# Re-ordering the first stage of a hybrid attention block: who sums the adaLN columns, who scales x, and where the gate's sums stand

## The chip, the cores and the metric

The kernel runs on one core of one Trainium2 chip. A core has a matrix engine (TensorE, PE in the profile), three engines for elementwise work (VectorE or DVE, ScalarE or ACT, GpSimd or POOL), and SyncE (SP), whose queue issues every DMA of this kernel. The engines run beside each other and are ordered by semaphores; each engine takes its own instructions strictly in the order in which the program wrote them. The metric is device time in microseconds. The kernel before takes 991.84 us, the median of 3 runs (989.53 to 992.6).

## The reference

One layer on x (1024 tokens by 1024 channels, float32), with a condition vector c of 1024 numbers:

```
ada = c @ w_ada + b_ada;  shift, scale, gate = split(ada, 3)
h = rms_norm(x, norm_w) * (1 + scale) + shift
cq, ckv, k_rope, gate_a, q_b, k_b, v_b, f_b, gate_b, mg_a, mg_b = split(h @ w_in)
branch A: latent attention from rms_norm(cq) @ w_uq and rms_norm(ckv) @ w_ukv, rotary part, chunk mask
branch B: forgetting attention from q_b, k_b, v_b, f_b, causal
merged = sigmoid(mg_a) * (y_a @ w_branch_a) + sigmoid(mg_b) * (y_b @ w_branch_b)
out = x + gate * (merged @ w_out)
```

What the change touches is the first two lines (shift and scale, the normalised and modulated h) and the third part of ada, the gate, which is needed only at the very end.

## The kernel before

Every float32 product is made of three products of a float32r high part and a low part (`hi*hi`, `hi*lo`, `lo*hi`), so each operand is split: ScalarE rounds to the high part, and the low part is a subtraction. h is held transposed, as 8 blocks of 128 channels by 1024 tokens (`hT_hi`, `hT_lo`, index `kt`).

The first stage (`phase0`) loads x in 8 tiles of 128 tokens, squares them with a sum per token, takes a reciprocal square root on VectorE for two tiles at a time (`rsqrt`: 11 small instructions, each needing the one before), and scales the tiles with it (`scale`). Seven of the eight tiles are scaled by GpSimd (L281), one by VectorE (L284). TensorE transposes each scaled tile (`turn`), and ScalarE copies the banks into `xT` (`evac`, L309).

For each channel block the shift and the scale are sums of 1024 products of c with a column of `w_ada`. With the weight's columns on the partitions, such a sum is one 128x1024 multiplication with c, laid along the free dimension of every partition (`cb`), and a sum along it (`ada_cols`). On VectorE it is one instruction (L339). On GpSimd it is the multiplication alone (L342), and ScalarE sums the product later (L344). Before the change the scale's sum of each block is VectorE's and the shift's sums of blocks 2 to 7 are GpSimd's and ScalarE's. The shift of blocks 0 and 1 is a matrix product of TensorE with rows on the partitions (`ada_rows`). `cb` is made by TensorE from a diagonal (`broadcast_c`) and copied by VectorE (L404). `gain` (L348, L349) turns the sums into the block's two per-channel factors `gs`. With them ScalarE writes the high part of h (`high`, L355), VectorE modulates `xT` in place (`modulate`, L359) and subtracts (`low`, L365). Then TensorE does 24 products of 128x424 for the block (`products`, 8 token tiles by 3 parts, into the banks cq_s, cq_o, cq_f, cq_t).

The order of work is written out by hand. In the loop over blocks, iteration `kt` does for block `kt + 1` the sums, the gain and the high part, and for block `kt` modulate, low and the products. The weights of the loads come from a pool of equal pieces of on-chip memory (`Slots`): a load waits, on SP's queue, until the last reader of the piece that it reuses is done.

The gate's 8 sums (`gate_sum`, 128 columns each) use the same form. Before the change they stand at the end of `phase0` and in `latents`: four multiplied by GpSimd (L932) and summed by ScalarE (L936), four by VectorE (L939). `gate_row` transposes the 8 columns to a row and stores it, during `g2q`, the queries of branch A.

After `phase0` come `latents` (the second latent's products, ckv, and their norms), `krope`, `g2q`, then `g2k` (keys and values of branch A, four pairs of token tiles `sp`), the attention of 16 heads, and `output`. From `latents` on, TensorE's time is filled by a planner: `fill_to(t)` puts in products of GEMMs that only have to be done in time (among them branch B's, bank `b`) until the estimated time t.

Of the kernel before, what the change touches and what calls it, by code (L numbers as in the profile page):

```python
# [19 lines left out]
P = 128  # L20
# [21 lines left out]
class Slots:  # L42
    """Equal pieces of SBUF, taken and given back by hand; the one given back longest ago goes first."""
# [31 lines left out]
class Net:  # L75
# [162 lines left out]
    # ------------------------------------------------------------ phase 0  # L238
    def phase0(self):
# [27 lines left out]
        def square(st, engine="a"):  # L267
            junk, a = Hs.get([P, 512], F32, f"junk{st}"), ssq[:, st:st + 1]
            if engine == "a":
                nc.scalar.activation(junk.bitcast(BF16), xs[st], AF.Square, accum_out=a)  # L270
            else:
                nc.vector.scalar_tensor_tensor(out=junk.bitcast(BF16), in0=xs[st], scalar=1.0, in1=xs[st], op0=ALU.mult,
                                               op1=ALU.mult, accum_out=a)
            Hs.put(junk)

        def scale(pair, between=iter(()), engines="pd"):
            a, b = pair
            r = self.rsqrt(ssq[:, a:b + 1], 2, D, f"x{a}", between)
            for i, (st, e) in enumerate(zip(pair, engines)):
                if e == "p":  # L280
                    nc.gpsimd.tensor_scalar(out=xs[st], in0=xs[st], scalar1=r[:, i:i + 1], scalar2=0.0, op0=ALU.mult,  # L281
                                            op1=ALU.add)
                else:
                    nc.vector.tensor_scalar(out=xs[st], in0=xs[st], scalar1=r[:, i:i + 1], scalar2=None, op0=ALU.mult)  # L284
# [20 lines left out]
        def evac(st, engines):  # L305
# [5 lines left out]
        def broadcast_c():  # L311
            """c along the free dimension of every partition, through a diagonal and a product with ones."""
            ones = Hs.get([P, P], F32, "ones")
            nc.gpsimd.memset(ones, 1.0)
            pc = self.bank("s", "cb")
            for g in range(2):
                diag = Hs.get([P, 4, P], F32, f"diag{g}")
                for i in range(4):
                    rc = 4 * g + i
                    nc.vector.tensor_scalar(out=diag[:, i], in0=self.ident, scalar1=col(rc), scalar2=None, op0=ALU.mult)  # L320
                for i in range(4):
                    rc = 4 * g + i
                    self.mm(pc[:, rc * P:(rc + 1) * P], ones, diag[:, i], True, True)
                Hs.put(diag)
            Hs.put(ones)
            return pc

        def ada_rows(kt, bank):
            """The shift of a block whose rows lie on the partitions."""
# [6 lines left out]
        def ada_cols(kt, e, engine="d"):  # L336
            w, a = wada[kt][e], acc[:, kt, e:e + 1]
            if engine == "d":
                nc.vector.scalar_tensor_tensor(out=w, in0=w, scalar=1.0, in1=self.cb, op0=ALU.mult, op1=ALU.mult,  # L339
                                               accum_out=a)  # L340
            elif engine == "p":
                nc.gpsimd.tensor_tensor(out=w, in0=w, in1=self.cb, op=ALU.mult)  # L342
            else:
                nc.scalar.activation(w, w, AF.Copy, accum_out=a)  # L344
# [12 lines left out]
        def modulate(kt, sts=range(ST), engine="d"):  # L357
            c = slice(sts[0] * P, (sts[-1] + 1) * P)
            (nc.vector if engine == "d" else nc.gpsimd).tensor_scalar(  # L359
                out=xT[:, kt, c], in0=xT[:, kt, c], scalar1=gs[:, kt, 1:2], scalar2=gs[:, kt, 0:1],  # L360
                op0=ALU.mult, op1=ALU.add)
# [16 lines left out]
        def modulated(kt, sts):  # L378
            high(kt, sts)
            modulate(kt, sts)  # L380
            low(kt, sts)

# [3 lines left out]
        load(0)  # L386
        load_cq(0, 0)
# [5 lines left out]
        pc = broadcast_c()  # L393
# [18 lines left out]
        wh, wl = U.get([P, 2, 424], F32R, "hi_cq0"), U.get([P, 2, 424], F32R, "lo_cq0")
        nc.scalar.copy(wh[:, 0], cqw[0][:, 0])
        ada_cols(0, 1)
        gain(0, a0)
        high(0, range(4))
        square(6, "d")
        square(7, "d")
        nc.gpsimd.tensor_tensor(out=wl[:, 0], in0=cqw[0][:, 0], in1=wh[:, 0].bitcast(F32), op=ALU.subtract)
        modulate(0, range(4))  # L420
        low(0, range(4))
        self.cqw.append((wh, wl))
        turn(4, "tt")
        evac(4, "aa")
        turn(5, "of")
        evac(5, "aa")
        high(0, (4, 5))
        accs = [self.bank("s", f"cq_s{i}") for i in range(2)]
# [3 lines left out]
        load(2)  # L432
        load_cq(1)
        load(3)
        nc.sync.dma_start(self.misc_raw[:, 0:t["misc"].shape[1]], t["misc"])
        nc.sync.dma_start(self.pos, t["pos"])
        a0 = ada_rows(1, "t")
        products(0, range(4), (2, 1))

        def between():  # L440
            yield
            modulate(0, (4, 5))
            low(0, (4, 5))
            yield

        nc.scalar.copy(wh[:, 1], cqw[0][:, 1])
        nc.gpsimd.tensor_tensor(out=wl[:, 1], in0=cqw[0][:, 1], in1=wh[:, 1].bitcast(F32), op=ALU.subtract)
        U.put(cqw[0])
        ada_cols(2, 0, "p")
        ada_cols(1, 1)  # L450
        gain(1, a0)
        scale((6, 7), between(), "pd")
        high(1, most)
        banks[4], banks[5] = self.bank("o", "cq_o"), self.bank("f", "cq_f")
        products(0, (4, 5), (0, 1))
        modulate(1, most)
        low(1, most)
        products(1, most, (0, ))
        products(0, (4, 5), (2, ))
        products(1, most, (1, ))  # L460
        turn(7, "tt")
        turn(6, "tt")
        products(1, most, (2, ))
        ada_cols(2, 0, "a")
        wh, wl = U.get([P, 2, 424], F32R, "hi_cq1"), U.get([P, 2, 424], F32R, "lo_cq1")
        nc.scalar.copy(wh, cqw[1])
        evac(7, "aa")
        load(4)
        load_cq(2)
        ada_cols(2, 1)  # L470
        gain(2)
        evac(6, "aa")
# [3 lines left out]
        banks[6], banks[7] = self.bank("t", "cq_t0"), self.bank("t", "cq_t1")  # L476
        ada_cols(3, 0, "p")
        load(5)
        for kt in range(2):
            high(kt, last)  # L480
        high(2)
        for kt in range(2):
            modulate(kt, last)
            low(kt, last)
        for kt in range(2):
            products(kt, last)
        ada_cols(4, 0, "p")
        load_cq(3)
        load(6)
        for kt in range(2, KT):  # L490
# [9 lines left out]
            if kt in (3, 5):  # L500
                self.cqw.append(self.split(cqw[(kt + 1) // 2], f"cq{(kt + 1) // 2}"))
            if kt == 3:
                load(7)
            if kt == 4:
                self.kvw = [self.load_w(t["w_ckv"][:, 4 * i:4 * i + 4], [P, 4, 256], f"ckv{i}") for i in range(2)]
            if kt == 5:
                self.gate_load((0, 1))
                self.gate_sum((0, 1), "p")
            if kt == 6:
                self.gate_load((2, 3))  # L510
                self.gate_sum((0, 1), "a")
                self.gate_sum((2, 3), "p")
            if kt == 7:
                self.gate_load((4, 5))
# [1019 lines left out]
```

## Time and profile before

| | |
|---|---|
| median of the runs | 991.84 us (989.53 to 992.6) |
| the profiled execution, span from the first to the last instruction | 989.3 us |
| PE busy | 954.5 us (96%) |
| VectorE busy | 659.8 us (67%) |
| ScalarE busy | 475.7 us (48%) |
| GpSimd busy | 250.8 us (25%) |
| DMA | 123.95 MB, mean 125 GB/s |

The profile gives the profiled execution's span and no separate device time for it; the span is 0.2 us below the fastest run. Busy shares are averages over stages with different limits, so the first stage has to be read by itself: a table of stretches of time, then each engine's instructions in order of time with the idle time before each and what ended it.

### The profile page before, as it was taken

How to read it: one execution, taken by the hardware profiler on the slowest of the kernel's cores; microseconds unless marked ns; L12 is line 12 of the kernel's file. 1: busy time of each engine (PE TensorE's matmuls, PEld its weight loads, DVE VectorE, ACT ScalarE, POOL GpSimd, SP SyncE). 2: the span in 40 equal slices, each digit the busy share in tenths (PEclk: the TensorE clock that was granted, in tenths of full speed). 3: DMA queues.
4: the chain of work that ended last, by engine and by line, in shares of the span. 5: the costliest groups of instructions: out<-in, count | busy, mean ns of one | idle time of the engine just before them, and what ended most of it. 6: DMA issues, size and time to landing. Idle time of an engine off the chain costs nothing.

```text
span 989.3 us, 15335 instructions
## 1 busy us (share of the span) xinstructions
PE 954.5 (96%) x5550; PEld 833.1 (84%) x5550; DVE 659.8 (67%) x1399; ACT 475.7 (48%) x962; POOL 250.8 (25%) x279
## 2 busy tenths in 40 slices
PE   6479999999999999999999999999999999999998
PEld 6379999999998888888888888888888888887887
DVE  6997787676734766757667667677676767495222
ACT  6347653344334655655646566566565644143000
POOL 4843222220001222221223233333332220045000
PEclk9889999999999999999999999999999999999999
DMA  9733113346485223424224232231321554643321
GB/s 345 285 128 131 52 55 107 124 150 221 155 251 149 67 95 84 139 66 109 84 65 119 77 108 66 86 109 65 118 87 45 181 181 148 228 148 126 100 92 64
DMA packets 80700, 123.95 MB, mean 125 GB/s; under 512 B 5896, under 2 KB 47504, under 8 KB 80624
## 3 DMA queue, kind: packets, MB, share of 16 engines
q1 hardware_dynamic: 80624, 122.96, 38.1%
q8 instruction: 44, 0.72, 0.3%
q14 instruction: 32, 0.26, 0.1%
HBM read 87.29 MB, written 35.66 MB: 124 GB/s over the span
## 4 chain that ended last, share of the span: by engine, by line
PE 85%; DVE 8%; DMA 4%; issue 1%; ACT 1%; SPq 0%; POOL 0%; ACTq 0%; DVEq 0%; POOLq 0%
PE f L127 31%; PE b L127 12%; PE out L127 9%; PE s L127 8%; PE o L127 7%; PE pt L136 6%; PE q L127 3%; PE ckv L127 2%; PE kv L127 2%; DVE hT_lo L1046 1%; DVE hT_lo L365 1%; DMA ks_u<-ka_d 1%; DVE wada_u L339 1%; PE cq_s L127 1%; DVE xT L359 1%
## 5 line engine op out<-in xcount | busy, mean ns | idle before, releaser
L1240 ACT CAST pp_u<-pt 128x512 fp32r<-128x512 f32 x192 | 92.1, 480 | 181.6 <-PE pt L136 167.8
L1241 DVE TENSOR_TENSOR pp_u<-pt,pp_u 128x512 fp32r<-128x512 f32 x192 | 106.6, 556 | 79.2 <-ACT pp_u L1240 77.1
L127 PE MATMUL f<-hT_hi,hi_f_u 128*128 128x512 f32 x384 | 153.6, 400 | 0.0
L127 PE MATMUL f<-hT_hi,lo_f_u 128*128 128x512 f32 x384 | 153.4, 400 | 0.0
L127 PE MATMUL f<-hT_lo,hi_f_u 128*128 128x512 f32 x384 | 153.2, 399 | 0.0
L127 PE MATMUL s<-k_u,q_u 96*128 96x512 f32 (+6 forms) x480 | 116.4, 361 | 0.7 <-ACT p_h L1220 0.7
L127 PE MATMUL b<-hi_b_u,hT_hi 128*128 128x256 f32 x384 | 109.6, 285 | 0.0
L127 PE MATMUL b<-hi_b_u,hT_lo 128*128 128x256 f32 x384 | 108.6, 283 | 0.0
L127 PE MATMUL b<-lo_b_u,hT_hi 128*128 128x256 f32 x384 | 108.6, 283 | 0.0
L1224 POOL TENSOR_SCALAR p_u<-p_u,rs 128x640 f32<-128x640 f32 (+1 forms) x64 | 65.2, 1018 | 164.4 <-DVE rs L1223 95.9
L1224 POOL TENSOR_SCALAR p_h<-p_h,rs 128x128 f32<-128x128 f32 (+1 forms) x64 | 38.6, 603 | 245.5 <-DVE rs L1223 205.7
L1214 DVE TENSOR_REDUCE nm<-s 128x1 f32<-128x128 f32 (+7 forms) x128 | 97.0, 758 | 4.4
L127 PE MATMUL o<-pp_u,v_u 128*128 128x512 f32 (+7 forms) x384 | 94.2, 340 | 0.0
L127 PEld LDWEIGHTS f<-hT_hi,lo_f_u 128*128 128x128 f32 x384 | 72.4, 189 | 11.9
L127 PEld LDWEIGHTS f<-hT_lo,hi_f_u 128*128 128x128 f32 x384 | 72.5, 189 | 11.2
L127 PEld LDWEIGHTS f<-hT_hi,hi_f_u 128*128 128x128 f32 x384 | 72.5, 189 | 11.1
L127 PEld LDWEIGHTS s<-k_u,q_u 96*128 96x128 f32 (+2 forms) x480 | 76.7, 190 | 6.1 <-ACT p_h L1220 1.2
L127 PEld LDWEIGHTS o<-pp_u,v_u 128*128 128x128 f32 (+1 forms) x384 | 61.8, 161 | 19.6
L127 PEld LDWEIGHTS b<-lo_b_u,hT_hi 128*128 128x128 f32 x384 | 73.6, 192 | 0.3
L127 PEld LDWEIGHTS b<-hi_b_u,hT_hi 128*128 128x128 f32 x384 | 73.6, 192 | 0.3
L127 PEld LDWEIGHTS b<-hi_b_u,hT_lo 128*128 128x128 f32 x384 | 73.6, 192 | 0.0
L136 PEld LDWEIGHTS pt<-ident,p_u 128*128 128x128 f32 x416 | 52.7, 140 | 16.6
(319 smaller groups left out, 2072.0 us busy)
## 6 DMA issues: line engine op xcount, KB each, us to landing
raw_f_u<-in_w_t SPq DMA_DIRECT2D x24, 512.0 KB
wada_u<-in_w_ada SPq DMA_DIRECT2D x16, 512.0 KB
mg_d<-th_h SPq DMA_DIRECT2D x32, 256.0 KB
mg_h<-mg_d SPq DMA_DIRECT2D x32, 256.0 KB
raw_b_u<-in_w_b SPq DMA_DIRECT2D x12, 512.0 KB
x_u<-in_x SPq DMA_DIRECT2D x8, 512.0 KB
raw_wg_u<-in_w_gate SPq DMA_DIRECT2D x8, 512.0 KB
va_d<-vhl_u SPq DMA_DIRECT2D x8, 512.0 KB
```

The costliest lines, as they stand in the source:

```text
L127: self.nc.tensor.matmul(out, lhsT=l, rhs=r, start=start, stop=stop)
L136: self.nc.tensor.transpose(out=out, in_=in_, identity=self.ident)
L339: nc.vector.scalar_tensor_tensor(out=w, in0=w, scalar=1.0, in1=self.cb, op0=ALU.mult, op1=ALU.mult, accum_out=a)
L359: (nc.vector if engine == "d" else nc.gpsimd).tensor_scalar(out=xT[:, kt, c], in0=xT[:, kt, c], scalar1=gs[:, kt, 1:2], scalar2=gs[:, kt, ...
L365: nc.vector.tensor_tensor(out=lo[:, kt, c], in0=xT[:, kt, c], in1=hi[:, kt, c].bitcast(F32), op=ALU.subtract)
L1046: nc.vector.tensor_tensor(out=self.hT_lo[x], in0=mA[c1][:, x[2]], in1=self.hT_hi[x].bitcast(F32), op=ALU.subtract)
L1214: nc.vector.tensor_reduce(out=nm, in_=sv, axis=AX.X, op=ALU.max, negate=True)
L1224: nc.gpsimd.tensor_scalar(out=p[:, 0:w], in0=p[:, 0:w], scalar1=rs, scalar2=0.0, op0=ALU.mult, op1=ALU.add)
L1240: nc.scalar.copy(ph[:, c0:], pt[:, c0:])
L1241: nc.vector.tensor_tensor(out=pl[:, c0:], in0=pt[:, c0:], in1=ph[:, c0:].bitcast(F32), op=ALU.subtract)
```

## The change

- c's row is laid into `cb` by a DMA with a repeated source row (new input `c_row`); `broadcast_c` and its copy go.
- All shift and scale sums are VectorE's, except block 0's shift (`ada_rows` on TensorE). They are written two blocks ahead of the block's products.
- VectorE scales all 8 tiles of x; all 8 squares are ScalarE's. The low parts of the first weights are VectorE's too, so no GpSimd instruction is left in `phase0` but a memset.
- ScalarE modulates `xT` (Identity with scale and bias, as for the high part) everywhere but for block 0's first six tiles.
- Tiles 6 and 7 of x are scaled, transposed and copied earlier, before block 1's sums.
- The transposes that only keep TensorE's clock up go from 16 to 32.
- The 8 gate sums leave `phase0` and `latents`. They are VectorE's, two behind each pair of `g2k`, with c's row loaded a second time (`cb2`) and the weights loaded one pair ahead. `gate_row` and the bias move into the attention, at head 2, step 0.

```diff
-        def scale(pair, between=iter(()), engines="pd"):
+        def scale(pair):
...
+                nc.vector.tensor_scalar(out=xs[st], in0=xs[st], scalar1=r[:, i:i + 1], scalar2=None, op0=ALU.mult)
...
+            if engine == "a":
+                nc.scalar.activation(xT[:, kt, c], xT[:, kt, c], AF.Identity, scale=gs[:, kt, 1:2], bias=gs[:, kt, 0:1])
+                return
...
+        self.cb = U.get([P, D], F32, "cb")
+        nc.sync.dma_start(self.cb, t["c_row"].broadcast_to([P, D]))
...
-        warm(16, self.ident)
-        scale((0, 1), engines="pp")
+        warm(32, self.ident)
+        scale((0, 1))
         turn(0, "s")
         turn(1, "tt")
...
         a0 = ada_rows(0, "o")
+        evac(2)
+        square(6)
+        ada_cols(0, 1)
+        gain(0, a0)
+        load(2)
+        evac(3)
...
+        high(0, range(4))
+        scale((4, 5))
+        modulate(0, range(4), "d")
         low(0, range(4))
...
+        scale((6, 7))
...
         products(0, range(4), (2, 1))
+        turn(6, "tt")
+        evac(6)
+        turn(7, "tt")
+        modulate(0, (4, 5), "d")
+        low(0, (4, 5))
+        products(0, (4, 5))
+        ada_cols(1, 0)
+        ada_cols(1, 1)
+        gain(1)
+        high(1, most)
+        modulate(1, most, "a")
         nc.scalar.copy(wh[:, 1], cqw[0][:, 1])
+        evac(7)
...
         for kt in range(2, KT):
-            if 2 < kt < KT - 2:
-                ada_cols(kt + 2, 0, "p")
+            if kt + 2 < KT:
+                ada_cols(kt + 2, 0)
+                ada_cols(kt + 2, 1)
+                gain(kt + 2)
             if kt + 1 < KT:
-                ada_cols(kt + 1, 0, "a")
-                ada_cols(kt + 1, 1)
-                gain(kt + 1)
-                high(kt + 1)
-            modulate(kt)
-            low(kt)
+                low(kt + 1)
+            if kt in (2, 4):
+                self.cqw.append(self.split(cqw[kt // 2 + 1], f"cq{kt // 2 + 1}"))
+            if kt + 2 < KT:
+                high(kt + 2)
+                modulate(kt + 2, engine="a")
...
+                self.cb = self.U.get([P, D], F32, "cb2")
+                nc.sync.dma_start(self.cb, t["c_row"].broadcast_to([P, D]))
+                self.gate_load((0, 1))
                 for sp in range(4):
                     self.g2k(sp)
+                    self.gate_sum((2 * sp, 2 * sp + 1))
+                    if sp < 3:
+                        self.gate_load((2 * sp + 2, 2 * sp + 3))
                     self.fill_to(self.pe_time + 6500)
```

## Rows read from the trace of the kernel before

**Rows 1.** Stretches: start:end, length, busy us by engine, PE clock, DMA share, GB/s

```profile
10.50:22.00 11.50, 8.88 (x62) 7.99 (x61) 8.76 (x28) 7.35 (x15) 7.42 (x6) 0.85 1.02 384
22.00:50.00 28.00, 13.50 (x83) 11.85 (x81) 27.44 (x35) 11.95 (x20) 23.12 (x10) 0.89 0.79 292
50.00:58.20 8.20, 8.09 (x32) 7.73 (x33) 8.10 (x17) 4.76 (x7) 0.00 (x0) 0.74 0.31 104
58.20:70.40 12.20, 7.90 (x42) 7.42 (x40) 12.17 (x8) 2.98 (x5) 11.06 (x4) 1.00 0.55 189
87.50:206.00 118.50, 118.39 (x990) 117.84 (x989) 93.36 (x279) 63.59 (x126) 34.56 (x52) 1.00 0.30 98
206.00:272.00 66.00, 66.00 (x466) 62.02 (x466) 46.35 (x118) 27.47 (x49) 4.39 (x5) 1.00 0.48 173
272.00:885.00 613.00, 610.67 (x3331) 514.31 (x3330) 407.97 (x826) 329.46 (x694) 149.92 (x179) 1.00 0.37 114
```

**Rows 2.** TensorE in order of time: start, us, instructions [idle before, releaser]

```profile
18.91 2.51 PE L127 MATMUL pada<-vec,wada_u 128*128 128x64 f32 x16
50.11 1.08 PE L127 MATMUL cq_t<-hi_cq_u,hT_lo 128*128 128x424 f32 x2 [9.14 <-DVE hT_lo L365]
53.10 1.48 PE L127 MATMUL cq_s<-hi_cq_u,hT_hi 128*128 128x424 f32 x4
70.46 1.04 PE L127 MATMUL cq_s<-hi_cq_u,hT_lo 128*128 128x424 f32 x4 [4.36 <-DVE hT_lo L365]
78.27 0.93 PE L127 MATMUL cq_s<-hi_cq_u,hT_hi 128*128 128x424 f32 x4
82.91 0.35 PE L127 MATMUL cq_s<-hi_cq_u,hT_hi 128*128 128x424 f32 x1
87.47 0.28 PE L127 MATMUL ckv<-hi_ckv_u,hT_hi 128*128 128x256 f32 x1
```

**Rows 3.** VectorE in order of time, not held by GpSimd

```profile
33.55 0.75 DVE L284 TENSOR_SCALAR x_u<-x_u,y_x 128x1024 f32<-128x1024 f32 x1
50.76 1.22 DVE L339 SCALAR_TENSOR_TENSOR wada_u<-wada_u,cb_u 128x1024 f32<-128x1024 f32 x1
52.16 0.81 DVE L359 TENSOR_SCALAR xT<-xT,gs 128x1024 f32<-128x1024 f32 x1
53.00 1.23 DVE L365 TENSOR_TENSOR hT_lo<-xT,hT_hi 128x1024 fp32r<-128x1024 f32 x1
54.14 1.22 DVE L339 SCALAR_TENSOR_TENSOR wada_u<-wada_u,cb_u 128x1024 f32<-128x1024 f32 x1
57.53 1.10 DVE L116 TENSOR_TENSOR lo_cq_u<-raw_cq_u,hi_cq_u 128x424 fp32r<-128x424 f32 x2
```

**Rows 4.** VectorE in order of time, the same shapes and one column, while GpSimd works

```profile
38.66 3.40 DVE L339 SCALAR_TENSOR_TENSOR wada_u<-wada_u,cb_u 128x1024 f32<-128x1024 f32 x1
42.12 2.15 DVE L349 SCALAR_TENSOR_TENSOR gs<-ada,b,vec 128x1 f32<-128x1 f32 x1
64.16 2.97 DVE L359 TENSOR_SCALAR xT<-xT,gs 128x1024 f32<-128x1024 f32 x1
67.17 3.24 DVE L365 TENSOR_TENSOR hT_lo<-xT,hT_hi 128x1024 fp32r<-128x1024 f32 x1
```

**Rows 5.** GpSimd in order of time

```profile
14.87 2.22 POOL L281 TENSOR_SCALAR x_u<-x_u,y_x 128x1024 f32<-128x1024 f32 x2 [1.94 <-ACT xT L309]
58.27 11.06 POOL L932 TENSOR_TENSOR raw_wg_u<-raw_wg_u,cb_u 128x1024 f32<-128x1024 f32 x4 [8.49 <-DMA raw_wg_u<-in_w_gate]
```

**Rows 6.** VectorE and ScalarE at the start and in block 2, in order of time

```profile
8.38 0.17 DVE L88 TENSOR_SCALAR v_x<-xssq 128x2 f32<-128x2 f32 x1 [1.96 <-ACT junk_h L270]
10.36 0.16 DVE L96 SCALAR_TENSOR_TENSOR y_x<-a_x,y_x 128x2 f32<-128x2 f32 x1
52.28 1.24 ACT L355 ACTIVATE hT_hi<-xT,gs 128x1024 fp32r<-128x1024 f32 x1 [5.69 <-DVE gs L349]
```

**Rows 7.** Waits in the keys' stage; waits of SP's own queue (us in total, times, longest)

```profile
ACT kv L833 <- DVE vhl_u L831: 10.1, 8, 3.3
SPq L102 <- PE o L127: 27.6, 7, 16.7
```

**Rows 8.** Chain that ended last, from 206 us: start, us, what

```profile
265.89 15.13 PE b L127 x126
```

More of the change, by code (lines that the diff above doesn't have):

```diff
@@ L265, in load_cq, with square @@
             nc.sync.dma_start(cqw[gi][:, k], t["w_cq"][:, 2 * gi + k.start:2 * gi + k.stop])
[L267 to L273, printed above, removed]
+        def square(st):
+            junk = Hs.get([P, 512], F32, f"junk{st}")
+            nc.scalar.activation(junk.bitcast(BF16), xs[st], AF.Square, accum_out=ssq[:, st:st + 1])
             Hs.put(junk)
-        def scale(pair, between=iter(()), engines="pd"):
+        def scale(pair):
             a, b = pair
[L278 to L284, printed above, removed]
+            r = self.rsqrt(ssq[:, a:b + 1], 2, D, f"x{a}")
+            for i, st in enumerate(pair):
+                nc.vector.tensor_scalar(out=xs[st], in0=xs[st], scalar1=r[:, i:i + 1], scalar2=None, op0=ALU.mult)
         def warm(n, src):
@@ L309, in evac @@
                 (nc.scalar.copy if e == "a" else nc.vector.tensor_copy)(xT[:, 4 * j:4 * j + 4, cols], src)
[L311 to L326, printed above, removed]
         def ada_rows(kt, bank):
@@ L334, in ada_rows, with ada_cols @@
             return pa[:, 0:1]
-        def ada_cols(kt, e, engine="d"):
+        def ada_cols(kt, e):
             w, a = wada[kt][e], acc[:, kt, e:e + 1]
[L338 to L344, printed above, removed]
+            nc.vector.scalar_tensor_tensor(out=w, in0=w, scalar=1.0, in1=self.cb, op0=ALU.mult, op1=ALU.mult, accum_out=a)
         def gain(kt, a0=None):
@@ L376, in products @@
                     product(kt, st, e)
[L378 to L381, printed above, removed]
         self.wg = {}
@@ L431, in phase0 @@
         products(0, range(4), (0, ))
-        load(2)
-        load_cq(1)
         load(3)
+        load_cq(2)
         nc.sync.dma_start(self.misc_raw[:, 0:t["misc"].shape[1]], t["misc"])
         nc.sync.dma_start(self.pos, t["pos"])
-        a0 = ada_rows(1, "t")
         products(0, range(4), (2, 1))
[L440 to L444, printed above, removed]
+        turn(6, "tt")
[3 more added lines that the diff above has]
+        low(0, (4, 5))
+        banks[4], banks[5] = self.bank("o", "cq_o"), self.bank("f", "cq_f")
+        products(0, (4, 5))
[4 more added lines that the diff above has]
+        modulate(1, most, "a")
         nc.scalar.copy(wh[:, 1], cqw[0][:, 1])
-        nc.gpsimd.tensor_tensor(out=wl[:, 1], in0=cqw[0][:, 1], in1=wh[:, 1].bitcast(F32), op=ALU.subtract)
+        evac(7)
+        nc.vector.tensor_tensor(out=wl[:, 1], in0=cqw[0][:, 1], in1=wh[:, 1].bitcast(F32), op=ALU.subtract)
         U.put(cqw[0])
[L449 to L456, printed above, removed]
-        low(1, most)
[L458 to L464, printed above, removed]
+        load(4)
+        low(1, most)
+        products(1, most)
         wh, wl = U.get([P, 2, 424], F32R, "hi_cq1"), U.get([P, 2, 424], F32R, "lo_cq1")
[L466 to L469, printed above, removed]
+        ada_cols(2, 0)
         ada_cols(2, 1)
         gain(2)
-        evac(6, "aa")
+        load(5)
+        banks[6], banks[7] = self.bank("t", "cq_t0"), self.bank("t", "cq_t1")
+        for kt in range(2):
+            high(kt, last)
+            modulate(kt, last, "a")
+        nc.scalar.copy(wh, cqw[1])
+        for kt in range(2):
+            low(kt, last)
+        for kt in range(2):
+            products(kt, last)
         nc.vector.tensor_tensor(out=wl, in0=cqw[1], in1=wh.bitcast(F32), op=ALU.subtract)
@@ L475, in phase0 @@
         self.cqw.append((wh, wl))
[L476 to L480, printed above, removed]
-        high(2)
[L482 to L487, printed above, removed]
+        high(2)
+        modulate(2, engine="a")
+        ada_cols(3, 0)
+        ada_cols(3, 1)
+        gain(3)
         load_cq(3)
         load(6)
+        low(2)
+        high(3)
+        modulate(3, engine="a")
         for kt in range(2, KT):
-            if 2 < kt < KT - 2:
-                ada_cols(kt + 2, 0, "p")
+            if kt + 2 < KT:
+                ada_cols(kt + 2, 0)
+                ada_cols(kt + 2, 1)
+                gain(kt + 2)
             if kt + 1 < KT:
-                ada_cols(kt + 1, 0, "a")
-                ada_cols(kt + 1, 1)
-                gain(kt + 1)
-                high(kt + 1)
-            modulate(kt)
-            low(kt)
-            if kt in (3, 5):
-                self.cqw.append(self.split(cqw[(kt + 1) // 2], f"cq{(kt + 1) // 2}"))
+                low(kt + 1)
[4 more added lines that the diff above has]
+                modulate(kt + 2, engine="a")
+            if kt == 2:
+                load(7)
             if kt == 3:
-                load(7)
-            if kt == 4:
                 self.kvw = [self.load_w(t["w_ckv"][:, 4 * i:4 * i + 4], [P, 4, 256], f"ckv{i}") for i in range(2)]
-            if kt == 5:
-                self.gate_load((0, 1))
-                self.gate_sum((0, 1), "p")
             if kt == 6:
[L510 to L514, printed above, removed]
                 self.kvs = [self.split(w, f"ckv{i}") for i, w in enumerate(self.kvw)]
```

58 lines of the change are left out of this document (18 added, 40 removed).

## The prediction

> **What bounds the kernel now.** Look at the table of stretches first, because the page's averages hide the answer. From 87.5 us on TensorE is busy 118.39 of 118.50 us, then 66.00 of 66.00, then 610.67 of 613.00, all at a granted clock of 1.00 [rows 1]. Whatever comes before 87.5 us and ends earlier moves the whole rest forward; whatever the change saves or adds on another engine behind 87.5 us is beside a full TensorE. So read the first stage alone. There VectorE is busy 27.44 of 28.00 us and 12.17 of 12.20 us, while TensorE works less than half of the one and two thirds of the other [rows 1]. The next view is TensorE in order of time: it stands 9.14 us and 4.36 us before products, both times until VectorE has a block's low part [rows 2]. VectorE bounds the stage.
>
> The third view says why VectorE is so full. Compare the same instruction twice: the sum takes 1.22 us at 50.76 and 3.40 us at 38.66, the modulation 0.81 and 2.97, the low part 1.23 and 3.24, and an instruction of one column takes 2.15 us [rows 3, 4]. GpSimd tells them apart. It has no busy time from 50.0 to 58.2, where everything is short, and 11.06 of 12.20 us from 58.2 to 70.4, where one block's four steps fill 12.2 us instead of the 3.38 from one sum's start to the next at 50.76 and 54.14 [rows 1, 3, 4]. DMA does not tell them apart: its share is 0.31 and 0.55 there, far from the 1.02 of 10.5 to 22 us [rows 1].
>
> The Trainium skill, "SBUF — State Buffer", section "Who interferes with whom", gives the reason: VectorE and GpSimd share one pair of memory ports, as an exclusive lock for a whole instruction, and a VectorE instruction with two SBUF inputs, or a copy or tensor_scalar in a two-port mode, blocks against it. The trace agrees (1.22 against 3.40 us); by that rule all the stretching goes with GpSimd's last instruction, and by a half-and-half reading only part of it.
>
> **The change part by part.** All GpSimd arithmetic leaves the stage, so I price VectorE with the unheld rows [rows 3]: two sums and a gain 2.6 us (1.14 from a sum's start to its end, twice, and 0.26 up to 52.16), a low part 1.14, a scaled tile 0.75, a weight's two low parts 1.10. ScalarE takes 1.24 us for a block of 1024 columns, high part and modulation alike [rows 6]. Then I walk the new order, every engine in its own order.
>
> Opening: the first reciprocal root ends at 10.5 as now (8.38 to 10.52, 2.14 us [rows 6]). VectorE scales two tiles to 12.0, does the next root and two tiles to 15.7; GpSimd ends them at 17.1 now [rows 5]. Tile 3's transposes end near 16.8, block 0's shift on TensorE takes up to 2.5 [rows 2], its gain comes at 19.6. Then VectorE has tiles 4 and 5 (3.6 us, to 23.3) and block 0's modulation, low part and weight (1.7, to 25.0). The root of tiles 6 and 7 waits about 1 us for ScalarE, which squares tile 7 behind tile 4's copies; both tiles are scaled at 29.6, low parts of tiles 4 and 5 done at 30.3. This is the new wait of the change: VectorE's whole queue stands behind it, block 1's sums first.
>
> Blocks 1 to 3: block 1's sums to 32.9. ScalarE's high part, modulation and weight copy follow to 35.4 and hold VectorE about 2 us, low part at 36.9. Block 2's sums to 39.5, low parts of the last tiles and weights to 41.3, block 3's sums to 43.9, block 2's low part at 45.0.
>
> The loop: 2.6 + 1.14 = 3.74 us of VectorE a block, 4.84 with a weight's split. Low parts come at 48.7, 53.5, 57.3 and 62.1, and for block 7, behind ScalarE's last two steps (2.5 us after 61.0), at 64.6. TensorE needs 4.64 us a block (78.27 to 82.91 [rows 2]), and a low part only in the last third of it. From 45.0 blocks 2 to 6 end at 46.6, 51.2, 55.8, 60.5 and 65.1, always just behind VectorE, and block 7 (4.56) at 69.7. The first ckv product now starts at 87.47 [rows 2]. Removed: 17.8 us. VectorE and TensorE are nearly level in the loop, which is why more cannot come from it.
>
> Clock: after the waits of 9.14 and 4.36 us TensorE ran at its lower level; the 8 products from 50.11 to 53.10 took 0.37 us each, against 4.64 / 24 = 0.19, and the clock of that stretch is 0.74 [rows 1, 2]. Such a run cost about 12 x 0.18 = 2.2 us. In the new order TensorE waits some 2 to 3 us at a time between 17 and 36; I count half of one such run, 1.1 us (ends: 0, if block 2's low part is awaited anyway, and 8.2, below).
>
> DMA: c's row adds 0.5 MB behind 4.2 MB of x and the first weights. At 384 GB/s [rows 1] that is 1.4 us, there near 14 us and needed at 15.7: cost 0 to 1 us, taken as 0. The weights of blocks 2 to 7 are all in by about 42 us (15.9 MB at that rate), each ahead of its sum; the last two wait in SP's queue for pieces freed near 32 and 38, and are needed at 53 and 58.
>
> Edits at nothing: the diagonal for c, its products and 16 more idle transposes lie before the first scaled tile at 11. The gate's sums in the latents leave VectorE and ScalarE while TensorE is full, so removing them gives 0 (TensorE's idle time there, 0.1 us, is the most).
>
> Gate sums behind the keys: 8 x 1.22 = 9.8 us on VectorE, which is idle 66.0 - 46.35 = 19.7 us in that stretch, and GpSimd works 4.39 us of it [rows 1, 3]. TensorE covers it as long as VectorE is late by less than the bank ahead. A pair's two sums (2.4 us) can land before a low part of v and hold ScalarE's next step, which already waits 10.1 us in all for VectorE, 3.3 at worst, with TensorE at 66.00 of 66.00 [rows 1, 7]. Between 0 and 2.4 for each of four pairs, 0 is nearest to that row: 0.3 in all. The 4.7 MB of loads join 173 GB/s there, well under 384. The moved row of the gate costs one transpose and a few tenths of VectorE in the attention: 0.2.
>
> Sum: -17.8 + 1.1 + 0.3 + 0.2 = -16.2. The profiled execution spans 989.3, so 973.1; the median of the runs lies 2.5 above that span, so the time to be measured is 991.8 - 16.2 = 975.6.
>
> **The rivals.** Half is lost in hand-offs: every product before block 2 (48 of them) runs at the lower clock, 48 x 0.17 = 8.2 us, or the opening chain of root, scale, transpose, copy, square is as much longer. For it: the clocks 0.85 and 0.89 [rows 1]. Against: in the loop TensorE is fed without gaps and any such run ends. Time 983.8.
>
> More is gained: TensorE is never late for block 2, and the lower load of VectorE and ScalarE shortens the latents' opening. TensorE could begin block 2 at 41 by its high part and end block 7 at 69.2, with no lower clock: 991.8 - 18.3 - 3 = about 970, the 3 for an opening shorter by the waits on ScalarE (1 and 2 us). Against: VectorE needs to 64.6 for the last low part.
>
> The stretching isn't GpSimd's: if it came with the stage's other traffic, VectorE would keep it and have more to do: 7 more tile scalings and 7 shift sums (7 x 0.75 + 7 x 1.22 = 13.8 [rows 3]) against some 11 removed (seven modulations at 0.84, two squares and a copy at 1.22, the diagonal). Time 991.8 + 3 = 995. Against it stand 8.2 us of short instructions beside 12.2 of long ones, with GpSimd off and on.
>
> Slower through the keys: SP takes its queue in order, so a gate load that waits for its piece holds back the stores and weights behind it, and VectorE, at a sum whose weights have not landed, holds k's scaling, ScalarE's copies of bank b, and so TensorE. One wait of SP for a piece reached 16.7 us [rows 7]. TensorE is covered for one bank of 48 products, 5.8 us (126 of them take 15.13 [rows 8]). Two such waits cost 2 x 10.9 = 21.8: 991.8 - 16.2 + 21.8 = 997.4. It decides from 16.2 us of uncovered waits on. Against: the loads are issued one pair, some 14 us, ahead, and SP waits that long now without TensorE being idle.
>
> **How the numbers follow.** Forecast 0.64 (973 to 979), half lost 0.17, more gained 0.07: together 0.88 for faster by over 0.3% (3 us, about what a measurement of this kernel can tell from no change). Keys 0.07 and stretching 0.05: of these 0.08 slower and 0.04 within 0.3%, where they only eat the gain. The range reaches from 969 (more gained, with a us of scatter) to 985 (half lost, with a us): 0.86 of the cases lie in it.
>
> **What would show it.** In the new trace VectorE's sums take 1.2 us throughout the first stage and GpSimd has nothing there; block 2's last products start near 45 and the first ckv product near 70; in the loop TensorE waits less than 1 us a block; from there to the end the time is as long as now within 2 us. The prediction is wrong if the first ckv product starts after 79, if instructions of VectorE are still held to 2 us or more, or if TensorE is idle for more than 3 us between 206 and 272 of the old count.

## The result, and the profile after

The changed kernel takes 978.16 us (median of 4 runs, 977.64 to 978.6) against 990.98 for the kernel before in the same measurement (4 runs, 989.53 to 992.6): a ratio of 0.9873, interval 0.9846 to 0.99, so 12.8 us gained. The forecast was 975.6 and a gain of 16.2. The profiled execution spans 976.3 us, 13.0 less than the 989.3 before.

First the table of stretches of the kernel after, the counterpart of [rows 1]; columns as there (PE, PEld, DVE, ACT, POOL busy, granted clock, DMA share, GB/s).

```profile
22.00:36.00 14.00, 10.05 (x51) 8.98 (x52) 9.53 (x27) 7.52 (x13) 0.00 (x0) 0.81 1.03 406
36.00:69.70 33.70, 33.65 (x174) 32.36 (x174) 29.47 (x55) 25.50 (x35) 2.05 (x7) 1.00 0.39 128
69.70:193.00 123.30, 123.10 (x1028) 122.63 (x1027) 95.24 (x276) 65.09 (x128) 36.22 (x57) 1.00 0.33 110
193.00:260.00 67.00, 64.70 (x454) 60.60 (x453) 52.17 (x132) 25.44 (x46) 0.00 (x0) 1.00 0.60 216
260.00:872.00 612.00, 607.45 (x3296) 510.62 (x3296) 404.54 (x822) 328.44 (x691) 146.85 (x179) 1.00 0.36 112
```

The loop over blocks, once half empty on TensorE, is full: 33.65 of 33.70 us. The seven GpSimd instructions of that stretch are one memset and, from 67.14 on, small ones of the next stage. New holes lie in the keys (64.70 of 67.00, once 66.00 of 66.00) and behind them (4.55 us idle, once 2.33). TensorE in order of time names them, with the lines that answer to [rows 2].

```profile
17.35 1.90 PE L127 MATMUL pada<-vec,wada_u 128*128 128x64 f32 x16
22.61 3.65 PE L136 MATMUL xt<-ident,x_u 128*128 128x128 f32 x16 [3.36 <-DVE x_u L276]
35.77 1.04 PE L127 MATMUL cq_s<-hi_cq_u,hT_hi 128*128 128x424 f32 x4 [2.85 <-ACT hi_cq_u L417]
46.40 0.55 PE L127 MATMUL cq_t<-hi_cq_u,hT_lo 128*128 128x424 f32 x2
69.75 0.28 PE L127 MATMUL ckv<-hi_ckv_u,hT_hi 128*128 128x256 f32 x1
259.68 0.58 PE L127 MATMUL b<-hi_b_u,hT_hi 128*128 128x256 f32 x1 [2.30 <-DVE bv_u L830]
278.01 0.63 PE L136 MATMUL kt<-ident,ks_u 128*128 128x128 f32 x4
370.51 0.27 PE L136 MATMUL pgT<-ident,gcol 128*8 128x128 f32 x1 [2.01 <-DVE gcol L885]
```

The first ckv product starts at 69.75, 17.72 earlier than in [rows 2]. Its start marks the end of the first stage, and "ckv" followed by a time means it from here on. The two waits for a low part (9.14 and 4.36) are gone. VectorE shows why; these rows of the kernel after answer to [rows 3, 4].

```profile
43.85 1.22 DVE L336 TENSOR_TENSOR hT_lo<-xT,hT_hi 128x1024 fp32r<-128x1024 f32 x1
44.99 1.22 DVE L313 SCALAR_TENSOR_TENSOR wada_u<-wada_u,cb_u 128x1024 f32<-128x1024 f32 x1
46.13 1.22 DVE L313 SCALAR_TENSOR_TENSOR wada_u<-wada_u,cb_u 128x1024 f32<-128x1024 f32 x1
47.41 0.21 DVE L318 SCALAR_TENSOR_TENSOR gs<-ada,b,vec 128x1 f32<-128x1 f32 x1
47.53 1.22 DVE L336 TENSOR_TENSOR hT_lo<-xT,hT_hi 128x1024 fp32r<-128x1024 f32 x1
```

All 15 sums of the stage take 1.22 us (before up to 3.40 in [rows 4]), the instruction of one column with two inputs 0.21 (before 2.15), and a block costs VectorE 3.68 us from low part to low part. GpSimd has a memset in the loop and no arithmetic of the stage.

To see what was given back, cut both executions at the same instructions (first ckv, first kv, first kt product, first scores, first out) and compare each part. The last column is TensorE's idle time, length less busy time.

| part | before | after | difference | idle, before and after |
|---|---|---|---|---|
| start to ckv | 87.47 | 69.75 | -17.72 | |
| ckv to kv | 122.78 | 122.64 | -0.14 | 0.11, 0.20 |
| kv to kt (keys) | 82.73 | 85.62 | +2.89 | 1.04, 2.32 |
| kt to scores | 5.22 | 5.22 | 0 | 0, 0 |
| scores to out (heads) | 598.09 | 601.71 | +3.62 | 3.08, 5.99 |
| out to end | 93.01 | 91.36 | -1.65 | 3.74, 3.70 |

The sum is -13.0. From the first ckv product to the end the changed kernel is 4.7 us longer. In the keys, 1.3 of the 2.9 is idle time, and the rest is clock: behind the wait of 2.30, thirteen products of bank b took 0.21 us each instead of 0.12, at a granted clock of 0.50, the lower of its two levels (columns as in the first table):

```profile
260.00:262.50 2.50, 2.50 (x13) 2.50 (x13) 1.43 (x3) 0.00 (x0) 0.00 (x0) 0.50 0.98 344
```

The last line of the table is clock too: the output ran at a mean clock of 0.98 before and 1.00 after, for the same work. No row says why.

### The profile page after: what moved, and what is told of

The parts are those of the page before. It is cut to its first block, busy times and chain, and to the rows that moved or that the text cites. A ratio compares the mean times of both kernels' runs of the same rounds, so it can differ in the third digit from the quotient of the medians.

```text
span 976.3 us, 15256 instructions
## 1 busy us (share of the span) xinstructions
PE 950.1 (97%) x5534; PEld 829.2 (85%) x5534; DVE 642.2 (66%) x1408; ACT 477.0 (49%) x955; POOL 203.4 (21%) x259
## 4 chain that ended last, share of the span: by engine, by line
PE 62%; DVE 3%; DMA 2%; issue 1%; ACT 0%; SPq 0%; ACTq 0%; DVEq 0%
PE f L127 31%; PE out L127 9%; PE s L127 8%; PE o L127 7%; PE pt L136 6%; DMA raw_f_u<-in_w_br 1%; DVE hT_lo L986 1%; DVE mg_h L979 1%; PE kt L136 1%; PE qt L136 1%; DMA mg_h<-mg_d 1%; DVE lo_f_u L116 1%; ACT p_u L1160 0%; ACT q_u L1096 0%; ACT hi_f_u L115 0%
## 5 line engine op out<-in xcount | busy, mean ns | idle before, releaser
L127 PEld LDWEIGHTS f<-hT_hi,lo_f_u 128*128 128x128 f32 x384 | 72.4, 189 | 11.9
L127 PEld LDWEIGHTS f<-hT_lo,hi_f_u 128*128 128x128 f32 x384 | 72.4, 189 | 11.5
```

The lines of the kernel that those rows point to most:

```text
L127: self.nc.tensor.matmul(out, lhsT=l, rhs=r, start=start, stop=stop)
```

## The experiments

The theory after the result has three parts. First, GpSimd's arithmetic stretched VectorE and taking it away is the gain. Second, the keys lose because two gate sums stand ahead of work that TensorE waits for. Third, the heads lose because the gate's bias addition stands behind VectorE's softmax work. The rival to the first is that the new order is the gain; to the others, that the time is lost there anyway, whatever VectorE does. Each experiment is the changed kernel with one edit, unless another is named, and is called by its number.

**Does GpSimd hold VectorE?** Two kernels add idle GpSimd work to the changed kernel, products (e9) and memsets (e10), on tiles that nobody else uses while it runs; in both traces no instruction waits for one of them.

```diff
+        for i in range(30):
+            nc.gpsimd.tensor_tensor(out=idle[2], in0=idle[0], in1=idle[1], op=ALU.mult)
```

> The changed kernel with 30 products of 128x512 on GpSimd from its start on, on pieces of memory that nobody else uses: no wait and no data joins them to the stage. Theory (an exclusive hold between GpSimd's reads and VectorE): VectorE's sums and low parts show 2 us and more while they run, the first ckv product comes 10 us or more after 69.75. Rival (the stretching came from the stage's other traffic or from waits): no change, 69.75 and 978.

```diff
+        for i in range(75):
+            nc.gpsimd.memset(idle[2], 1.0)
```

> The same with 75 fills of 128x512 on GpSimd, which write and read nothing. If the hold is between reads: VectorE's sums and low parts (two inputs in on-chip memory) stay at 1.2 us and at most the scalings and modulations by a per-partition factor are held; first ckv product before 73. If any instruction of GpSimd holds VectorE: as with the products, 10 us or more late.

One run of each: with the products 1002.24 us and ckv at 93.5, 23.7 later; with the memsets 985.94 and ckv at 76.8, 7.0 later (the kernel before on that chip: 993.37, one run). Now VectorE's groups from 10 to 70 us; columns: count, busy us, mean ns of one, idle before. First the changed kernel:

```profile
L313 DVE SCALAR_TENSOR_TENSOR wada_u<-wada_u,cb_u 128x1024 f32<-128x1024 f32 x15 | 17.8, 1220 | 0.7 <-DMA cb_u<-in_c_row 0.7
L276 DVE TENSOR_SCALAR x_u<-x_u,y_x 128x1024 f32<-128x1024 f32 x8 | 5.7, 751 | 0.1
L96 DVE SCALAR_TENSOR_TENSOR y_x<-a_x,y_x 128x2 f32<-128x2 f32 x12 | 1.9, 161 | 0.4
```

With GpSimd products:

```profile
L313 DVE SCALAR_TENSOR_TENSOR wada_u<-wada_u,cb_u 128x1024 f32<-128x1024 f32 x9 | 11.8, 1339 | 0.0
L276 DVE TENSOR_SCALAR x_u<-x_u,y_x 128x1024 f32<-128x1024 f32 x8 | 10.7, 1382 | 0.1
L96 DVE SCALAR_TENSOR_TENSOR y_x<-a_x,y_x 128x2 f32<-128x2 f32 x12 | 6.7, 557 | 0.4
```

With GpSimd memsets:

```profile
L313 DVE SCALAR_TENSOR_TENSOR wada_u<-wada_u,cb_u 128x1024 f32<-128x1024 f32 x15 | 17.8, 1219 | 0.0
L276 DVE TENSOR_SCALAR x_u<-x_u,y_x 128x1024 f32<-128x1024 f32 x8 | 8.3, 1072 | 0.1
L96 DVE SCALAR_TENSOR_TENSOR y_x<-a_x,y_x 128x2 f32<-128x2 f32 x12 | 1.9, 161 | 0.4
```

The products stretch all three forms; in order of time, small instructions of 0.16 alternate with ones of 1.11, so these were held for most of a GpSimd product (1353 ns in the mean). Of the nine sums only the first ran beside the products, and it took 2.29 us:

```profile
31.91 2.29 DVE L313 SCALAR_TENSOR_TENSOR wada_u<-wada_u,cb_u 128x1024 f32<-128x1024 f32 x1
```

The memsets stretch instructions with one tile as input, the scaling by one factor per token among them (751 to 1072 ns), and leave those with two tiles as inputs alone (1219 and 161 ns). That is the split which was expected, but the stage lost more by it than expected: ckv came at 76.8, not before 73. GpSimd's work alone, without any dependence, holds VectorE.

The rule in the Trainium skill, "SBUF — State Buffer", section "Who interferes with whom", draws just this line: an instruction of VectorE with two inputs in SBUF meets GpSimd where that reads, not where it only writes, while a tensor_scalar in a two-port mode meets it either way. The trace agrees: 161 against 557 ns, 161 against 161, and 751 against 1382 and 1072.

**How much of it for real work?** One kernel gives the shift sums of blocks 2 to 7 back to GpSimd and ScalarE (e8), one gives GpSimd the scaling of x (e7), one lets VectorE modulate (e6).

```diff
+            if kt >= 2 and e == 0:
+                nc.gpsimd.tensor_tensor(out=w, in0=w, in1=self.cb, op=ALU.mult)
+                nc.scalar.activation(w, w, AF.Copy, accum_out=a)
+                return
             nc.vector.scalar_tensor_tensor(out=w, in0=w, scalar=1.0, in1=self.cb, op0=ALU.mult, op1=ALU.mult, accum_out=a)
```

> The changed kernel with the shift's sums of blocks 2 to 7 by GpSimd (the product) and ScalarE (the sum), as before the change. Theory (GpSimd holds VectorE): 6 products of 2.4 to 3.3 us hold VectorE for about 12 us and take 6.9 us of sums off it: its sums show 2 us and more, the stage ends some 5 us later, 983. Rival (no hold): VectorE is shorter, TensorE bounds the stage, 977 to 978.

It took 990.58 us (10 runs, 987.54 to 993.25; ratio 1.0005, interval 0.9991 to 1.0019): the whole gain is gone by the medians. In its profile ckv starts at 81.35, 11.6 later, where the theory had 5. VectorE, then GpSimd, from 27 to 82 us of this kernel:

```profile
L317 DVE SCALAR_TENSOR_TENSOR wada_u<-wada_u,cb_u 128x1024 f32<-128x1024 f32 x8 | 11.8, 1483 | 0.0
L88 DVE TENSOR_SCALAR v_x<-xssq 128x2 f32<-128x2 f32 x1 | 2.4, 2378 | 1.4 <-ACT junk_h L269 1.4
```

```profile
L314 POOL TENSOR_TENSOR wada_u<-wada_u,cb_u 128x1024 f32<-128x1024 f32 x6 | 15.3, 2543 | 35.3 <-DMA wada_u<-in_w_ada 35.2
```

VectorE has six sums less to do (7.3 us at 1.22) and is still later. For GpSimd's 15.3 us, one instruction of two columns (0.16 elsewhere) took 2.38.

```diff
-                nc.vector.tensor_scalar(out=xs[st], in0=xs[st], scalar1=r[:, i:i + 1], scalar2=None, op0=ALU.mult)
+                nc.gpsimd.tensor_scalar(out=xs[st], in0=xs[st], scalar1=r[:, i:i + 1], scalar2=0.0, op0=ALU.mult, op1=ALU.add)
```

> The changed kernel with GpSimd scaling the 8 tiles of x. Theory (GpSimd holds VectorE, and takes 1.13 us a tile against 0.71): the opening is longer by 1 to 2 us, 979.5. Rival (GpSimd only takes 5.7 us of work off VectorE): 1 to 2 us shorter, 976.7.

It took 981.91 us (980.16 to 986.29; ratio 0.9918, interval 0.9886 to 0.995), ckv at 73.8: 4.1 later.

```diff
-            if engine == "a":
+            if engine == "x":
                 nc.scalar.activation(xT[:, kt, c], xT[:, kt, c], AF.Identity, scale=gs[:, kt, 1:2], bias=gs[:, kt, 0:1])
```

> The changed kernel with VectorE modulating everywhere instead of ScalarE. Theory (VectorE and TensorE nearly level): VectorE's queue is 6.5 us longer and about 2.5 us of its waits for ScalarE go, block 7's low part comes near 68.5 instead of 64.4, TensorE ends the stage 3 us later: 981.2. Rival 1 (TensorE alone bounds it): 978. Rival 2 (VectorE alone): 984.7.

It took 980.5 us (978.81 to 980.97; ratio 0.9894, interval 0.9879 to 0.9909), ckv at 72.4: 2.7 later. With VectorE at 3.68 us a block and TensorE at 4.64, another modulation (0.81 in [rows 3]) fits the plain blocks and not those with a weight's split; in its trace TensorE waits 0.5 to 0.8 us for a low part four times. The old order without GpSimd's arithmetic was not run, so how much the new order adds of its own is not shown.

**The gate's part alone (e5)**, on the kernel before: its 8 sums go behind the keys, the rest of the first stage stays.

```diff
-                self.gate_load((0, 1))
-                self.gate_sum((0, 1), "p")
...
+                    self.gate_sum((2 * sp, 2 * sp + 1))
+                    if sp < 3:
+                        self.gate_load((2 * sp + 2, 2 * sp + 3))
...
+        self.extra += [((2, 0), self.gate_row, ())]
```

> The kernel before with only the gate's part of the change: its 8 sums by VectorE behind the keys, its row at head 2; the first stage as before, without GpSimd's four gate products. Theory (GpSimd's products hold VectorE): the stretch that was 12.2 us a block falls to 3.4, the first ckv product comes near 81.5 instead of 87.5, and the keys and the row give back 3.5 and 2.0: about 990.5, no measurable change. Rival (the stretching has another cause, the gate's part only adds): 996.5.

It took 991.33 us (10 runs, 989.2 to 993.15; ratio 1.0005, interval 0.999 to 1.002). Its ckv starts at 82.4, 5.1 earlier than before: the 11.06 us of GpSimd of [rows 5] are gone, and with them TensorE's wait of 4.36, while the wait of 9.14, which lies beside GpSimd work that stays, is still there. Its keys then take 84.94 (+2.2) and its heads 602.23 (+4.1): the sums' new place costs what their going brought.

**Undoing the two waits.** The bias addition right behind the last sum (e1), the last two sums behind the next filling products (e2), and both (e3):

```diff
+                nc.vector.tensor_tensor(out=self.gcol, in0=self.gcol, in1=self.b_gate, op=ALU.add)
                 self.U.put(self.cb)
```

> The changed kernel with one edit: the addition of the gate's bias to the 8 sums stands right behind the last sum, not directly ahead of its transpose at head 2. Theory (VectorE's queue: the transpose waits 2.0 us for an addition that is queued behind VectorE's softmax work): that wait of TensorE goes and nothing takes its place, 2.0 us less than the changed kernel, near 976.2. Rival (TensorE would stand at this step anyway, for P's copies): the wait shows under another name, within 0.5 us of the changed kernel, 978.

```diff
-                    self.gate_sum((2 * sp, 2 * sp + 1))
                     if sp < 3:
+                        self.gate_sum((2 * sp, 2 * sp + 1))
                         self.gate_load((2 * sp + 2, 2 * sp + 3))
                     self.fill_to(self.pe_time + 6500)
+                self.gate_sum((6, 7))
```

> The changed kernel with one edit: the last two gate sums stand behind the products that follow the last pair of keys, not ahead of them. Theory (the two sums, 2.3 us, stand on VectorE ahead of the low part of branch B's v, which frees the bank that TensorE waits for): the 2.3 us wait goes, and with it the lower clock that follows it (13 products at 0.21 instead of 0.12 us, 1.2 us): 3.5 us less, near 974.7. Rival (the keys' stage is late by its 4.7 MB of added loads): the wait stays, 978.

> Both edits, the early addition and the last two sums behind the products. Theory: the two waits are independent, 5.5 us less than the changed kernel, near 972.7. Rival (one fill of TensorE covers either): 3.5 us less at most, 974.7.

979.47 us (977.76 to 980.47), 979.58 (978.96 to 982.18) and 979.3 (978.23 to 982.4), with ratios of 0.9876, 0.9884 and 0.9881 to the kernel before. None is faster than the changed kernel, and all three miss the time of the theory. Each wait did go. In the first the gate's transposition waits for nothing. In the other two bank b waits for nothing, and another wait stands instead. TensorE of e3:

```profile
278.28 0.63 PE L136 MATMUL kt<-ident,ks_u 128*128 128x128 f32 x4 [2.74 <-DMA ks_u<-ka_d]
```

Cut like the table above, e3 against the changed kernel is 1.2 later at ckv, 0.9 shorter from kv to kt, 1.5 longer from kt to the scores (at a clock of 0.75 behind the new wait) and 0.9 shorter in the heads.

**Copies first (e4).** The kernel of e3, and ScalarE rounds the weight's second half and copies the eighth transposed block before block 1's high part, against the waits of 2.85 (TensorE) and 2.59 (VectorE) that begin near 33 and end near 36.

```diff
         turn(7, "tt")
+        nc.scalar.copy(wh[:, 1], cqw[0][:, 1])
+        evac(7)
...
-        nc.scalar.copy(wh[:, 1], cqw[0][:, 1])
-        evac(7)
```

> Both edits, and in the first stage ScalarE rounds block 0's second weight and copies tile 7's transposes before block 1's high part and modulation, not behind them. In the trace of the changed kernel TensorE waits 2.9 us for that rounding (35.77) and then works without a gap up to the latents. Theory (TensorE bounds the stage from there on): it starts 1.0 to 1.5 us earlier and keeps that: near 971.5. Rival (VectorE bounds the loop): the products of block 2 wait for its low part instead, 972.7 as without this edit.

978.66 us (5 runs: 973.66, 976.63, 978.66, 979.25, 978.71; ratio 0.9857, interval 0.9835 to 0.9879). ckv comes at 68.7, 1.0 earlier. The profiled execution is the one of 973.66: its heads take 598.29, as before the change.

**Using VectorE's pause.** The last two sums and the bias addition go further back, into an idle stretch of VectorE of 4 us at the attention's start (e11); then the same with the copies first (e12).

```diff
         self.fill_to(self.pe_time + 10000)
+        self.gate_sum((6, 7))
+        self.nc.vector.tensor_tensor(out=self.gcol, in0=self.gcol, in1=self.b_gate, op=ALU.add)
+        self.U.put(self.cb)
         self.load_v(0)
```

> The changed kernel with the last two gate sums and the bias addition moved into VectorE's pause in front of the first head's operands, behind the third of V's low parts of branch b (in the run with both edits VectorE stood idle from 265.94 to 270.10 there; the two sums take 2.4). Theory: in that run the two sums, standing behind the fill, still kept the second of these low parts (262.13) some 2.5 us late, SP waited with its store for it until 263.2 and issued the load of the keys (ks_u) at 267.45, 1.2 us later behind the first ckv product than in the kernel before. With the pause used, ks_u is issued at the ckv product + 195.5, TensorE waits for it 1.0 to 1.8 instead of 2.7 and for nothing else in the stage, the first key transposition comes at the ckv product + 205.5 to 206.5 (before 205.5, changed kernel 208.3, both edits 207.4), gate transposition without a wait; time 976.5 to 977.5 against 978.2 of the changed kernel. Rival: what is won at the attention's start is lost again in waits of the late heads as in the runs before, and the time is 978.3 to 979.5.

> The same, and ScalarE makes the two copies of the first stage (the second half of the weights' high part, the eighth turned column block) right behind that turn, as in the run with the copies first, where the first ckv product came 1.0 earlier than in the changed kernel (68.7). Theory: both gains add: ckv product at 68.7, first key transposition at 274.2 to 275.2, time 975.5 to 976.5. Rival: one of the two is lost later and the time is that of the copies-first run, 978 to 979.

e11 took 978.33 us (6 runs, 974.12 to 982.09; ratio 0.9874, interval 0.9849 to 0.9899), e12 976.76 us (4 runs, 974.91 to 977.68; ratio 0.9855, interval 0.9836 to 0.9874). e12 has the lowest median of all kernels, 1.4 below the changed one, and the intervals overlap. The theory's number for the keys failed in both: the wait for the keys' load did not shrink to 1.0 to 1.8, it was 3.59 in e11 and 4.74 in e12, which came earliest:

```profile
277.35 1.09 PE L136 MATMUL kt<-ident,ks_u 128*128 128x128 f32 x4 [4.74 <-DMA ks_u<-ka_d]
```

**What holds the keys.** In the changed kernel the loss is the last pair's: the two sums stand right ahead of the low part of v for which bank b waits, and TensorE hardly waits for the first head's keys (0.03 us).

```profile
256.66 1.22 DVE L878 SCALAR_TENSOR_TENSOR raw_wg_u<-raw_wg_u,cb_u 128x1024 f32<-128x1024 f32 x1
257.80 1.22 DVE L878 SCALAR_TENSOR_TENSOR raw_wg_u<-raw_wg_u,cb_u 128x1024 f32<-128x1024 f32 x1
258.94 0.68 DVE L830 TENSOR_TENSOR bv_u<-b,bv_u 128x512 fp32r<-128x512 f32 x1
```

So e2, e3, e4, e11 and e12 moved that pair. For the wait that took its place, the traces point at the third pair. First the kernel before, VectorE then SP:

```profile
255.86 1.29 DVE L841 TENSOR_TENSOR kraw_h<-kraw_h,y_g2k 128x512 f32<-128x512 f32 x2
257.07 0.68 DVE L894 TENSOR_REDUCE bssq<-bsq_h 128x8 f32<-128x512 f32 x1
```

```profile
261.04 2.17 SPq L918 DMA_DIRECT2D kb_d<-bo_h  x4
282.82 0.46 SPq L1087 DMA_DIRECT2D ks_u<-ka_d  x1
```

The kernel after, VectorE then SP:

```profile
238.01 1.29 DVE L788 TENSOR_TENSOR kraw_h<-kraw_h,y_g2k 128x512 f32<-128x512 f32 x2
239.22 1.22 DVE L878 SCALAR_TENSOR_TENSOR raw_wg_u<-raw_wg_u,cb_u 128x1024 f32<-128x1024 f32 x1
240.36 1.22 DVE L878 SCALAR_TENSOR_TENSOR raw_wg_u<-raw_wg_u,cb_u 128x1024 f32<-128x1024 f32 x1
241.51 0.68 DVE L841 TENSOR_REDUCE bssq<-bsq_h 128x8 f32<-128x512 f32 x1
```

```profile
245.48 2.17 SPq L865 DMA_DIRECT2D kb_d<-bo_h  x4
268.85 0.47 SPq L1027 DMA_DIRECT2D ks_u<-ka_d  x1
```

Two sums stand between the scaling of branch A's keys and the norms of branch B's. The second half of B's keys is stored that much later: 173.57 us behind ckv before, 175.73 after, and 175.7 to 176.0 in all twelve experiments. That store opens a stretch in which the DMA engines hardly rest. The stretches of the kernel after, and then of e12, with clock, DMA share and GB/s at the end:

```profile
251.00:256.00 5.00, 5.00 (x44) 5.00 (x43) 3.88 (x15) 2.17 (x5) 0.00 (x0) 1.00 1.02 385
266.00:271.00 5.00, 5.00 (x44) 5.00 (x43) 0.69 (x1) 0.58 (x1) 0.00 (x0) 1.00 1.08 282
271.00:276.00 5.00, 5.00 (x44) 5.00 (x44) 2.89 (x4) 3.32 (x5) 0.00 (x0) 1.00 1.00 256
```

```profile
263.00:268.00 5.00, 5.00 (x44) 5.00 (x44) 3.26 (x8) 1.47 (x3) 0.00 (x0) 1.00 1.11 265
268.00:273.00 5.00, 4.61 (x39) 4.41 (x37) 2.90 (x4) 1.85 (x3) 0.00 (x0) 1.00 1.10 259
273.00:278.00 5.00, 0.65 (x3) 0.68 (x4) 0.00 (x0) 0.00 (x0) 0.00 (x0) 0.84 0.65 159
```

About 10 MB pass, the load of the first head's keys (ks_u) among the last. Issuing it earlier does not land it earlier: it is issued 22.0 us behind the first of these four stores in e6, 20.8 in e3 and 20.9 in e12, and the first kt product comes 31.0, 31.6 and 33.6 behind that store (31.9 before, 32.5 after); in e3 and e12 it waits for the load, in e6 it doesn't. So a DMA sets the end of the keys once VectorE no longer does. The wait for bank b lay beside it: e2, e3, e4, e11 and e12 don't have it and wait 2.7 to 4.7 for the load instead, and from kv to kt they take 84.7 to 86.7 us, the changed kernel, e1 and e5 to e10, which have it, 84.1 to 85.6, the kernel before 82.7. What is common to all thirteen is the store that comes about 2.2 us later. That the third pair is the cause is read off the traces; a kernel with that pair elsewhere was not run.

## Why the prediction was right, point by point

- **VectorE held by GpSimd: right.** The unheld prices gave the stage: ckv forecast at 69.7, seen at 69.75. Low parts were forecast to end at 45.0, 48.7, 53.5, 57.3, 62.1 and 64.6 and end at 45.07, 48.75, 53.45, 57.13, 61.83 and 64.51. The two GpSimd loads (+23.7 and +7.0 at ckv) and the shift sums given back (+11.6) show the cause. The rival that the stretching isn't GpSimd's falls, and so does that of half lost in hand-offs, which would have put ckv some 8 us later.
- **What limits the loop: half right.** The walk let VectorE set block 2 and TensorE follow. From 35.77 on TensorE has no gap at 4.64 us a block, and it reaches the products that need block 2's low part (ready at 45.07) at 45.13, so the last 34 us are TensorE's as much as VectorE's. With the copies first it comes there sooner and waits 0.48 for a low part.
- **The clock, +1.1: the size was right, and the profile of the result happened to escape it.** The run at a lower clock in the opening is there (0.81 from 22 to 36), where TensorE waits anyway (3.36 and 2.85). Behind the wait of 2.85 this profile ran at full clock; e1, e2, e3 and e11, whose first stage is the same and which wait 2.7 to 2.85 there, ran a stretch at the lower level behind it. The changed kernel, then e3:

```profile
36.00:39.00 3.00, 3.00 (x17) 2.95 (x17) 3.00 (x5) 2.93 (x7) 0.00 (x0) 1.00 1.01 383
```

```profile
38.00:40.50 2.50, 2.50 (x9) 2.31 (x8) 2.50 (x9) 2.41 (x4) 0.00 (x0) 0.50 0.89 334
```

  From the end of that wait to ckv they took 34.8 to 35.0 us, the changed kernel 34.0, and their ckv came at 69.9 to 70.9. So it is in part luck that the walk without this term met ckv to 0.1 us, and differences of up to 1.2 at ckv between two profiles are scatter.
- **The opening's waits: right in place.** ScalarE's rounding was priced at 2 us of VectorE and took 2.59. Its removal brought ckv 1.0 (e4) and 1.7 (e12) earlier than in the changed kernel's profile, and nothing that the medians show by itself. c's row was taken as free and held VectorE for 0.69.
- **Gate sums behind the keys: the mis-sized term.** Priced at +0.3, it is +2.9. The forecast took the bank ahead as cover for two sums on VectorE. It was not: TensorE waited 2.30 for bank b behind the last pair, and ran at the lower clock after it, 1.6 us more. Nor would the cover have been enough, because SP waits too: for a store, and behind it lies a stretch of DMA without slack that ends with the first head's keys. The slower rival had the right direction, with another mechanism and a price far too high: SP waited 3.9 us in all for pieces for the gate's loads, and no sum waited for its weights.
- **The moved row of the gate: mis-sized.** Priced at +0.2 for its work, it showed a wait of 2.01: its bias addition stood in VectorE's queue at a place where the transposition was due. Five profiles without that wait (e1, e3, e4, e11, e12) have heads of 598.3 to 602.2 us, mean 600.0; eight with it (after, e2, e5 to e10) 600.6 to 602.5, mean 601.9. So it cost about 1.9, less than the scatter of the first five, and no median shows its removal.
- **The rest behind ckv: taken as unchanged, and it was not.** The prediction's own sign, that from ckv to the end the time is as long as now within 2 us, failed: it is 4.7 longer.

By its own terms the forecast was -17.8 + 1.1 + 0.3 + 0.2; measured are -17.7, 0, +2.9 and about +1.9, and -0.1 from the rest of the heads (+3.62 less 1.9), ckv to kv (-0.14) and the output (-1.65), together -13.0. That the heads' rest and the output's clock nearly cancel is luck: neither was forecast.

What stays open is the scatter of the late heads. ScalarE's rounding of a late weight (raw_f_u) waits for its load, with the exponentials behind it: 1.49 us before, 2.29 in the fastest execution of the copies-first kernel, 2.33 in e5, 2.76 in e8, and 3.1 to 4.6 in the other ten profiles. The first three have no wait of TensorE for the exponential of the big tiles near 790, e8 has one of 0.45, and the ten have one of 0.8 to 1.2 (1.24 in the changed kernel, beside the 2.01 the heads' other new wait). ScalarE, first after, then copies first:

```profile
789.20 1.14 ACT L115 CAST hi_f_u<-raw_f_u 128x512 fp32r<-128x512 f32 x2 [3.76 <-DMA raw_f_u<-in_w_br]
```

```profile
784.06 1.14 ACT L115 CAST hi_f_u<-raw_f_u 128x512 fp32r<-128x512 f32 x2 [2.29 <-DMA raw_f_u<-in_w_br]
```

They go together; that the load is the cause was not tested, and executions of one kernel differ by up to 8 us (e11, 974.12 to 982.09).

## What to carry to other kernels

Compare one instruction's duration with the other elementwise engine on and off before handing that engine a share of the work; here the share cost more than it carried. When work moves to an engine with idle time, look at what its next instructions feed, SP's stores too, and follow the first of them to a stretch of full DMA or full TensorE. A wait that disappears without the time getting shorter was cover for a later one: find that before moving the next instruction.

## What the runs showed of the hardware that was not expected

- SP's issuing itself became slow in two kernels: four issues of q_u took 3.67 and 3.61 us in e11 and e12, 2.29 to 2.58 in the kernel before, after, e2, e3 and e4. The DMA engines' share from the store of B's keys to the first kt product is 0.97 to 1.00 in all seven, so full engines alone don't tell the two apart; the cause is open.
- The clock's cost follows a wait, but not each: the first head's opening products took 6.5 to 7.9 us at a clock of 0.63 to 0.78 in e2, e3, e11 and e12, behind waits of 2.7 to 4.7 for the keys, and 5.2 at 1.00 in e4, behind a wait of 3.3, as in the kernels without such a wait. In e5, e6 and e8 nothing was lost to the clock behind the wait of 2.3 for bank b that cost the changed kernel 1.6.
